# Projections ya and sb of a mixer formed with channels on partitions, with no transposition behind them

## The chip, the cores and the metric

The kernel runs on one core of a Trainium2 chip. The metric is the device time of one execution in microseconds, as the median of several runs. A core has TensorE for matrix products (PE in the profile, its weight loads PEld), VectorE (DVE), ScalarE (ACT), GpSimd (POOL) and SyncE (SP, which here only issues DMAs). Each takes its own instructions in order, and they wait for one another through semaphores.

## What is computed

Two blocks run one after the other on 256 tokens of width 1024, all in float32. The first is two layers of feed-forward, hybrid mixer, feed-forward; the second is one layer of attention and feed-forward. The change touches the mixer alone, which runs twice. Cut to what matters:

```python
def hybrid_mixer(u, ...):                      # u: 256 x 1024, normalised
    proj = u @ w_in                            # 1024 x 14336
    xa, ya, q, k, v, g, sb, sc, sh, gates = jnp.split(proj, cuts, axis=-1)
    xa = causal_depthwise_conv(xa, lru_conv_w) + lru_conv_b
    ha = rg_lru(xa, ...)                       # a linear recurrence along the tokens
    oa = (ha * jax.nn.gelu(ya)) @ w_lru_out
    ret = retention(q, k, v, positions)
    ob = (jax.nn.silu(g) * ret) @ w_ret_out
    oc = (sb * causal_depthwise_conv(sc * sh, sc_conv_w)) @ w_sc_out
    ga, gb, gc = jnp.split(jax.nn.sigmoid(gates), 3, axis=-1)
    return (ga * oa + gb * ob + gc * oc) @ w_out
```

The recurrence and the convolutions run along the tokens, channel by channel, and the results `ha * gelu(ya)` and `sb * conv(...)` are contracted over channels by the next weights. Both want the channels on the partitions and the tokens along the free axis.

## The kernel before

**Products in three parts.** Every float32 operand is held as a high part and a low part (`split`, L201 and L202, and for weights `convert`, L133 on ACT and L134 on DVE), and a product is three matmuls, high by high, high by low and low by high (`mm3`, L165 to L167). The weights come in 334 groups of 128 x 2048 by DMA into `raw` (three buffers), and are turned into `wh` and `wl` (five buffers each) in halves of 1024 columns.

**Projections with tokens on partitions.** `proj` takes one tile t of 128 tokens: the normalised activations `uh[t]`, `ul[t]`, which lie with the model width on partitions, are the stationary operand (128 x 128), and 512 columns of weights stream past them. Eight steps k over the width, three matmuls each, fill one PSUM bank `c` (two banks) of 128 tokens x 512 channels. The factor 1/rms of each token, `r2[t]`, is one number for each partition there, and is applied as the bank is read out.

**Turning to channels.** What is wanted with channels on partitions is turned. xa, sc and sh go through PE transposes (`transp`, L209). ya and sb go through `flip`: after the read-out into `yat` or `sbt`, DVE transposes 16 blocks for each 128 x 512, each of 32 rows by 4 x 32 columns (L224).

**Order.** The mixer goes: xa (four groups of weights), ya (four), sc and sh in two halves (eight), sb (four), the product with `w_lru_out` (four), the first gates, the product with `w_sc_out`, the second gates, then q, k, v and the retention. `later(n, fn)` holds work back until n steps of `mm3` more have been written; so `lru_half(0)` comes 8 steps and `lru_half(1)` 32 steps after ya, and the four strips of a `flip` come 5 (ya) or 28 (sb) steps after the read-out, two steps apart. `lru_half` makes a short convolution on ACT and DVE (`xc`, L446 and L448), then small float32 matmuls on it (L456), sigmoids (L459), the recurrence (L471), the product with ya (L473) and the split. From what is written a framework makes the final order of each engine's queue: it estimates when each instruction can start, and lets one that was written later go ahead of one that it takes to be still waiting. In the trace the conversions of weights run ahead of their use in this way.

Of the kernel before, what the change touches and what calls it, by code (L numbers as in the profile page):

```python
# [11 lines left out]
F32 = mybir.dt.float32  # L12
F32R = mybir.dt.float32r
I32 = mybir.dt.int32
AF = mybir.ActivationFunctionType
ALU = mybir.AluOpType
AX = mybir.AxisListType

P = 128
# [6 lines left out]
NEG = -1e30  # L26
CONV = 2
WSTEP = 2
WY = 5
WR = 6  # L30
WG = 8
WL0 = 8
WL1 = 32
WS0 = 5
WS1 = 12
WSB = 28
WMA = 14
WMB = 28
WMC = 18
# [6 lines left out]
S5 = 12  # L46
S6 = 32
WARM = 12
NRAW = 3
NW = 5  # L50
NGN = 3
# [21 lines left out]
def build(ctx: ExitStack, tc: tile.TileContext, a: dict, plan: list):  # L73
    nc = tc.nc
    V, A, G, T = nc.vector, nc.scalar, nc.gpsimd, nc.tensor

    def pool(name, bufs, **kw):
        return ctx.enter_context(tc.tile_pool(name=name, bufs=bufs, **kw))

    const = pool("const", 1)  # L80
    rawp = pool("raw", NRAW)
    wp = pool("w", NW)
# [5 lines left out]
    psC = pool("psc", 2, space=bass.MemoryType.PSUM)  # L88
# [12 lines left out]
    ident = const.tile([P, P], F32, name="ident")  # L101
# [1 line left out]
    G.memset(mhalf, -0.5)  # L103
    junk = const.tile([P, D], mybir.dt.bfloat16, name="junk")
    x = [const.tile([P, D], F32, name=f"x{t}") for t in range(2)]
    uh = [const.tile([P, 8, P], F32R, name=f"uh{t}") for t in range(2)]
    ul = [const.tile([P, 8, P], F32R, name=f"ul{t}") for t in range(2)]
    cst = const.tile([P, L, 12, 8], F32, name="cst")
    cos = const.tile([P, 2, P], F32, name="cos")
    sin = const.tile([P, 2, P], F32, name="sin")  # L110
# [1 line left out]
    lsz2 = const.tile([P, L, 8], F32, name="lsz2")  # L112
    tab = const.tile([33, 16], F32, name="tab")
    const.tile([P, 16], F32, name="even")
    r2 = [None, None]
    count = [0]
    pend = []
# [2 lines left out]
    def b4(name, dt=F32):  # L120
        return b4p.tile([P, D], dt, tag="b4", name=name)

    def b2(name, dt=F32):
        return b2p.tile([P, 512], dt, tag="b2", name=name)
# [4 lines left out]
    def tpbank(name="tp"):  # L129
        return psT.tile([P, 512], F32, tag="tp", name=name)  # L130
# [16 lines left out]
    def fetch(dst, src):  # L147
        with tc.issue_after(tail[0].ins if hasattr(tail[0], "ins") else tail[0]):
            nc.sync.dma_start(dst, src)
# [14 lines left out]
    def mm3(ps, xh, xl, wh, wl, first, last):  # L164
        T.matmul(ps, xh, wh, start=first, stop=False)  # L165
        T.matmul(ps, xh, wl, start=False, stop=False)  # L166
        T.matmul(ps, xl, wh, start=False, stop=last)  # L167
        count[0] += 1
        while pend and pend[0][0] <= count[0]:
            pend.pop(0)[1]()  # L170

    def later(n, fn):
        due = count[0] + n
        i = len(pend)
        while i and pend[i - 1][0] > due:
            i -= 1
        pend.insert(i, (due, fn))
# [22 lines left out]
    def split(hi, lo, src):  # L200
        A.copy(hi, src)  # L201
        V.tensor_tensor(lo, src, hi.bitcast(F32), ALU.subtract)  # L202
# [15 lines left out]
    def flip(dst, src, n, wait, done=None):  # L218

        sv = src[:, :n * P].rearrange("p (k n) -> p k n", n=P)  # L220

        def strip(q):
            for j in range(4):
                V.transpose(dst[32 * j:32 * j + 32, :, 32 * q:32 * q + 32], sv[32 * q:32 * q + 32, :, 32 * j:32 * j + 32])  # L224
            if q == 3 and done:
                done()

        for q in range(4):
            later(wait + q * WSTEP, lambda q=q: strip(q))
# [33 lines left out]
    def win(name, l, c0, n=512):  # L263
        kn = 2048 // n
        return [grp(name, l, k, kn, c0, n) for k in range(0, 8, kn)]

    def wout(name, l, k0, nk):
        return [grp(name, l, k, 2, 0, D) for k in range(k0, k0 + nk, 2)]

    def proj(gs, t, n=512, n0=0, nn=None):  # L270
        nn = n if nn is None else nn
        ps = psC.tile([P, 512], F32, tag="c", name="c")[:, :nn]
        kn = 2048 // n
        for k in range(8):
            wh, wl = gs[k // kn]
            sl = slice(n0, n0 + nn)
            mm3(ps, uh[t][:, k, :], ul[t][:, k, :], wh[:, k % kn, sl], wl[:, k % kn, sl], k == 0, k == 7)
        return ps

    def new_o():  # L280
# [2 lines left out]
    def acc_out(o, gs, xh, xl, first, last):  # L283
        for gi, (wh, wl) in enumerate(gs):
            for j in range(2):
                k = 2 * gi + j
                for n in range(2):
                    sl = slice(n * 512, n * 512 + 512)
                    mm3(o[:, sl], xh[:, k, :], xl[:, k, :], wh[:, j, sl], wl[:, j, sl],
                        first and k == 0, last and k == 2 * len(gs) - 1)  # L290
# [108 lines left out]
    def mixer(l, gpost, gpre):  # L399
        W = "w_mix_in"  # L400

        def chunk_tok(c0, n, cb):
            gs = [win(W, l, c0 + 512 * c) for c in range(n)]
            for t in range(2):
                for c in range(n):
                    cb(c, t, proj(gs[c], t))

        def chunks(c0, n, cb):
            for c in range(n):
                gs = win(W, l, c0 + 512 * c)  # L410
                for t in range(2):
                    cb(c, t, proj(gs, t))

        def ch(tile_):
            return tile_.rearrange("p (k s) -> p k s", s=S)
# [14 lines left out]

        wab = gp.tile([P, 2, 8, 64], F32, tag="gain", name="wab")
        fetch(wab, a["wab"][l])
        chunk_tok(0, 2, xa_cb)

        def col(row, k):
            return cst[:, l, row, k:k + 1]

        lru = []
        ya = [None, None]
# [35 lines left out]
            split(h, lo, rr)  # L475
            lru.append((h, lo))

        def ya_cb(c, t, ps):
            if ya[c] is None:
                ya[c] = ch(b4(f"ya{c}"))  # L480
            tmp = b2("yat")
            A.activation(tmp, ps, AF.Gelu_apprx_tanh, scale=r2[t])  # L482
            flip(ya[c][:, :, t * P:(t + 1) * P], tmp, 4, WY)

        chunks(1024, 2, ya_cb)
        later(WL0, lambda: lru_half(0))
        later(WL1, lambda: lru_half(1))

        pt = [None, None]
        for c in range(2):  # L490
            scs = [None, None]
            gs = win(W, l, 9216 + 512 * c)
# [4 lines left out]
            gs = win(W, l, 10240 + 512 * c)  # L497
# [4 lines left out]
        for c in range(2):  # L502
            z = ch(b4(f"z{c}"))
            for j in range(4):
                k = 4 * c + j
                A.activation(z[:, j, :], pt[c][:, j, :], AF.Copy, scale=col(SW + 2, k))
                for s in range(1, 3):
                    V.scalar_tensor_tensor(z[:, j, s:], pt[c][:, j, :S - s], col(SW + 2 - s, k), z[:, j, s:],
                                           ALU.mult, ALU.add)
            gs = win(W, l, 8192 + 512 * c)  # L510
            h, lo = ch(b4(f"sh{c}", F32R)), ch(b4(f"sl{c}", F32R))
            for t in range(2):
                tmp = b2("sbt")
                A.activation(tmp, proj(gs, t), AF.Copy, scale=r2[t])

                def cb(tp, z=z, h=h, lo=lo, sl=slice(t * P, (t + 1) * P)):
                    V.tensor_tensor(z[:, :, sl], tp, z[:, :, sl], ALU.mult)
                    split(h[:, :, sl], lo[:, :, sl], z[:, :, sl])
                sbT = b2("sbT").rearrange("p (k n) -> p k n", n=P)
                flip(sbT, tmp, 4, WSB, lambda cb=cb, sbT=sbT: cb(sbT))  # L520
            sco.append((h, lo))

        acc = [None, None]
# [137 lines left out]
        gs = wout("w_mix_out", l, 0, 8)  # L661
# [266 lines left out]
    warm = tpbank("warm")  # L928
    for i in range(WARM):
        T.transpose(warm[:, :P], ident, ident)  # L930
# [110 lines left out]
def _weights(inputs, plan):  # L1041
    w2 = inputs["w_in_2"]
    perm = np.arange(w2.shape[2])
    halves = np.arange(512).reshape(2, 4, 64).transpose(1, 0, 2).reshape(-1)
    for c in (0, 768, 1280):
        perm[c:c + 512] = c + halves
    src = dict(inputs)
    src["w_in_2"] = w2[:, :, perm]
    w = np.empty((NG, P, 2048), np.float32)
    for i, (name, l, k0, kn, c0, n) in enumerate(plan):  # L1050
        blk = src[name][l][k0 * P:(k0 + kn) * P, c0:c0 + n]
        w[i] = blk.reshape(kn, P, n).transpose(1, 0, 2).reshape(P, 2048)
    return w


def _program(inputs):
    import concourse.bacc as _bacc

    nc = _bacc.Bacc("TRN2", target_bir_lowering=False, num_devices=1)
    arrays = _layout(inputs)  # L1060
    args = {n: nc.dram_tensor(n, v.shape, mybir.dt.from_np(v.dtype), kind="ExternalInput").ap()
            for n, v in arrays.items()}
    args["wts"] = nc.dram_tensor("wts", (NG, P, 2048), F32, kind="ExternalInput").ap()
    args["out"] = nc.dram_tensor("out", (S, D), F32, kind="ExternalOutput").ap()
    plan = []
    with tile.TileContext(nc) as tc:
        build(tc, args, plan)
    arrays["wts"] = _weights(inputs, plan)
    return nc, arrays, plan
# [9 lines left out]
```

## Time and profile before

| what | value |
|---|---|
| median of 3 runs | 2027.7 us (2027.6 to 2027.93) |
| profiled execution: its time, its span | 2028.99 us, 2027.2 us |
| PE busy | 1972.9 us (97%), 9170 matmuls |
| DVE busy | 1668.2 us (82%) |
| ACT busy | 1037.3 us (51%) |
| weights read from HBM | 367.05 MB, mean 182 GB/s |

The span is the time from the first to the last instruction in the profile. A matmul's busy time overlaps that of the next, so how fast PE works is read from the distance between the starts of two matmuls rather than from their durations. PEclk is the share of full speed at which TensorE's clock was granted.

### The profile page before, as it was taken

How to read it: one execution, taken by the hardware profiler on the slowest of the kernel's cores; microseconds unless marked ns; L12 is line 12 of the kernel's file. 1: busy time of each engine (PE TensorE's matmuls, PEld its weight loads, DVE VectorE, ACT ScalarE, POOL GpSimd, SP SyncE). 2: the span in 40 equal slices, each digit the busy share in tenths (PEclk: the TensorE clock that was granted, in tenths of full speed). 3: DMA queues.
4: the chain of work that ended last, by engine and by line, in shares of the span. 5: the costliest groups of instructions: out<-in, count | busy, mean ns of one | idle time of the engine just before them, and what ended most of it. 6: DMA issues, size and time to landing. Idle time of an engine off the chain costs nothing.

```text
span 2027.2 us, 24429 instructions
## 1 busy us (share of the span) xinstructions
PE 1972.9 (97%) x9170; PEld 1623.8 (80%) x9170; DVE 1668.2 (82%) x2893; ACT 1037.3 (51%) x1384; POOL 58.5 (3%) x116
## 2 busy tenths in 40 slices
PE   9999999999999999999999999999999999999997
PEld 7778868788788888888887778887888888787886
DVE  7989789776877998988878995777789897679997
ACT  6444676444444543544466843454454445654553
POOL 0000000000010000000000000000010000010000
PEclk9999999999999999999999999999999999999999
DMA  6555533654445454555653546435545556424542
GB/s 250 192 208 198 187 134 137 244 189 166 166 160 212 173 207 181 198 197 187 239 190 107 183 184 220 169 115 199 205 166 208 198 207 207 161 94 149 220 183 102
DMA packets 56319, 369.72 MB, mean 182 GB/s; under 512 B 6582, under 2 KB 8886, under 8 KB 13704
## 3 DMA queue, kind: packets, MB, share of 16 engines
q1 hardware_dynamic: 56200, 368.16, 49.9%
q8 instruction: 72, 1.18, 0.2%
q14 instruction: 47, 0.39, 0.1%
HBM read 367.05 MB, written 1.08 MB: 182 GB/s over the span
## 4 chain that ended last, share of the span: by engine, by line
PE 65%; DVE 24%; ACT 4%; issue 3%; DMA 2%; POOL 0%; SPq 0%; DVEq 0%; POOLq 0%; ACTq 0%
PE c L165 13%; PE c L166 13%; PE c L167 13%; DVE ht L224 9%; DVE wl L134 8%; PE o L166 7%; PE o L167 7%; PE o L165 7%; DMA raw<-wts 2%; ACT wh L133 2%; DVE sbT L224 2%; DVE ya L224 2%; PE tp L209 2%; PE tp L456 1%; PE pv L762 1%
## 5 line engine op out<-in xcount | busy, mean ns | idle before, releaser
L134 DVE TENSOR_TENSOR wl<-raw,wh 128x1024 fp32r<-128x1024 f32 (+1 forms) x670 | 787.7, 1216 | 171.9 <-ACT wh L133 168.7
L133 ACT CAST wh<-raw 128x1024 fp32r<-128x1024 f32 (+1 forms) x670 | 670.0, 1046 | 336.4 <-PE c L167 163.6
L165 PE MATMUL c<-wh,uh 128*128 128x512 f32 (+1 forms) x1912 | 740.4, 387 | 14.4 <-DVE v L608 5.6
L166 PE MATMUL c<-wl,uh 128*128 128x512 f32 (+1 forms) x1912 | 734.9, 384 | 11.1 <-DVE wl L134 11.1
L167 PE MATMUL c<-wh,ul 128*128 128x512 f32 (+1 forms) x1912 | 734.3, 384 | 0.0
L165 PEld LDWEIGHTS c<-wh,uh 128*128 128x128 f32 x1912 | 363.2, 190 | 89.5 <-DVE v L608 6.5
L166 PEld LDWEIGHTS c<-wl,uh 128*128 128x128 f32 x1912 | 363.4, 190 | 82.5 <-DVE wl L134 12.6
L167 PEld LDWEIGHTS c<-wh,ul 128*128 128x128 f32 x1912 | 362.9, 190 | 71.1 <-issue 1.2
L224 DVE STREAM_TRANSPOSE ht<-sil 32x128 f32<-32x128 f32 (+1 forms) x768 | 223.9, 292 | 10.7
L224 DVE STREAM_TRANSPOSE ht<-sg 32x128 f32<-32x128 f32 x256 | 77.5, 303 | 3.5
L224 DVE STREAM_TRANSPOSE ht<-mh 32x128 f32<-32x128 f32 x256 | 77.5, 303 | 3.4
L195 POOL TENSOR_SCALAR ms<-ss 128x1 f32<-128x1 f32 x52 | 21.9, 421 | 1936.8 <-ACT junk L190 1915.6
L306 ACT ACTIVATE sil<-c,r 128x512 f32<-128x512 f32 (+1 forms) x48 | 31.3, 651 | 41.0 <-PE c L167 40.9
L311 DVE SCALAR_TENSOR_TENSOR sil<-c,r,sil 128x512 f32<-128x512 f32 (+1 forms) x48 | 33.7, 702 | 13.3 <-PE c L167 13.1
L224 DVE STREAM_TRANSPOSE ya<-yat 32x128 f32<-32x128 f32 x128 | 38.7, 302 | 6.0 <-ACT yat L482 4.3
L224 DVE STREAM_TRANSPOSE sbT<-sbt 32x128 f32<-32x128 f32 x128 | 38.8, 303 | 2.0
L197 POOL TENSOR_TENSOR r<-ms,mhalf 128x1 f32<-128x1 f32 x54 | 35.4, 656 | 4.5
L201 ACT CAST h2h<-ht 128x512 fp32r<-128x512 f32 x10 | 6.2, 623 | 52.2 <-DVE ht L224 52.2
L166 PE MATMUL o<-wl,h1h 128*128 128x512 f32 x80 | 31.4, 392 | 0.2 <-DVE wl L134 0.2
L166 PE MATMUL o<-wl,h4h 128*128 128x512 f32 x80 | 31.2, 390 | 0.0
L165 PE MATMUL o<-wh,h3h 128*128 128x512 f32 x80 | 31.2, 390 | 0.0
L166 PE MATMUL o<-wl,h3h 128*128 128x512 f32 x80 | 31.2, 390 | 0.0
(334 smaller groups left out, 2434.1 us busy)
## 6 DMA issues: line engine op xcount, KB each, us to landing
raw<-wts SPq DMA_DIRECT2D x332, 1024.0 KB, 4.8
tb<-row SPq DMA_DIRECT2D x8, 384.0 KB, 5.4
gain_ffn_post_g<-gains SPq DMA_DIRECT2D x4, 512.0 KB, 7.6
dec<-dec SPq DMA_DIRECT2D x4, 384.0 KB, 5.6
gain_ffn_pre_g<-gains SPq DMA_DIRECT2D x3, 512.0 KB, 8.5
x<-x SPq DMA_DIRECT2D x2, 512.0 KB, 5.7
raw<-wts SPq DMA_DIRECT2D x4, 256.0 KB, 5.5
raw<-wts SPq DMA_DIRECT2D x2, 512.0 KB, 6.4
```

The costliest lines, as they stand in the source:

```text
L133: A.copy(wh[:, sl], raw[:, sl])
L134: V.tensor_tensor(wl[:, sl], raw[:, sl], wh[:, sl].bitcast(F32), ALU.subtract)
L165: T.matmul(ps, xh, wh, start=first, stop=False)
L166: T.matmul(ps, xh, wl, start=False, stop=False)
L167: T.matmul(ps, xl, wh, start=False, stop=last)
L195: G.tensor_scalar(ms, ss, mul / n, mul * EPS, ALU.mult, ALU.add)
L197: G.tensor_tensor(r, ms, mhalf, ALU.pow)
L209: T.transpose(tp[:, j, :], src[:, (b + j) * P:(b + j + 1) * P], ident)
L224: V.transpose(dst[32 * j:32 * j + 32, :, 32 * q:32 * q + 32], sv[32 * q:32 * q + 32, :, 32 * j:32 * j + 32])
L306: A.activation(sil[t], ps, AF.Silu, scale=r2[t])
L311: V.scalar_tensor_tensor(sil[t], ps, r2[t], sil[t], ALU.mult, ALU.mult)
L456: T.matmul(ps[b:b + 64, j, :], wab[b:b + 64, g, 4 * c + j0 + j, :], xc[b:b + 64, j0 + j, :], start=True, stop=True)
```

## The change

For ya and sb the operands trade places: 128 columns of weights become the stationary operand, and 256 tokens (both tiles, from one buffer that now holds both) stream past. The result has channels on partitions. Each bank `c` then holds two blocks of 128 channels by 256 tokens. The factor 1/rms now varies along the free axis, so it is laid out once in each mixer as a row that is the same on all partitions (`rrow`), by a product of a matrix of ones with a diagonal. DVE applies it as it reads the bank out. `mm3c` counts as half a step, so the numbers given to `later` keep their sense.

```diff
-    uh = [const.tile([P, 8, P], F32R, name=f"uh{t}") for t in range(2)]
-    ul = [const.tile([P, 8, P], F32R, name=f"ul{t}") for t in range(2)]
+    uhb = const.tile([P, 2, 8, P], F32R, name="uh")
+    ulb = const.tile([P, 2, 8, P], F32R, name="ul")
+    uh, ul = [uhb[:, t] for t in range(2)], [ulb[:, t] for t in range(2)]
...
+    ones = const.tile([P, P], F32, name="ones")
+    G.memset(ones, 1.0)
+    rrow = const.tile([P, 2, P], F32, name="rrow")
...
+    def mm3c(ps, xh, xl, wh, wl, first, last):
+        T.matmul(ps, wh, xh, start=first, stop=False)
+        T.matmul(ps, wl, xh, start=False, stop=False)
+        T.matmul(ps, wh, xl, start=False, stop=last)
+        tick(0.5)
...
+    def scale_rows():
+        tp = tpbank("rb")
+        for t in range(2):
+            dg = b2("dg")[:, :P]
+            A.activation(dg, ident, AF.Copy, scale=r2[t])
+            T.matmul(tp[:, t * P:(t + 1) * P], ones, dg, start=True, stop=True)
+        A.copy(rrow.rearrange("p t n -> p (t n)"), tp[:, :2 * P])
+
+    def per_token(ps):
+        return rrow.unsqueeze(1).to_broadcast([P, 2, 2, P])
+
+    def proj_ch(gs, j0):
+        ps = psC.tile([P, 512], F32, tag="c", name="c").rearrange("p (j t n) -> p j t n", j=2, t=2)
+        for j in range(2):
+            sl = slice((j0 + j) * P, (j0 + j + 1) * P)
+            for k in range(8):
+                wh, wl = gs[k // 4]
+                mm3c(ps[:, j], uhb[:, :, k, :], ulb[:, :, k, :], wh[:, k % 4, sl], wl[:, k % 4, sl], k == 0, k == 7)
+        return ps
...
+        later(ROWS, scale_rows)
         chunk_tok(0, 2, xa_cb)
...
-        def ya_cb(c, t, ps):
-            if ya[c] is None:
-                ya[c] = ch(b4(f"ya{c}"))
-            tmp = b2("yat")
-            A.activation(tmp, ps, AF.Gelu_apprx_tanh, scale=r2[t])
-            flip(ya[c][:, :, t * P:(t + 1) * P], tmp, 4, WY)
-
-        chunks(1024, 2, ya_cb)
+        for c in range(2):
+            gs = win(W, l, 1024 + 512 * c)
+            ya[c] = ch(b4(f"ya{c}"))
+            for j in range(0, 4, 2):
+                y = ya[c][:, j:j + 2, :].rearrange("p j (t n) -> p j t n", n=P)
+                ps = proj_ch(gs, j)
+                V.tensor_tensor(y, ps, per_token(ps), ALU.mult)
+                A.activation(y, y, AF.Gelu_apprx_tanh)
...
-            for t in range(2):
-                tmp = b2("sbt")
-                A.activation(tmp, proj(gs, t), AF.Copy, scale=r2[t])
-
-                def cb(tp, z=z, h=h, lo=lo, sl=slice(t * P, (t + 1) * P)):
-                    V.tensor_tensor(z[:, :, sl], tp, z[:, :, sl], ALU.mult)
-                    split(h[:, :, sl], lo[:, :, sl], z[:, :, sl])
-                sbT = b2("sbT").rearrange("p (k n) -> p k n", n=P)
-                flip(sbT, tmp, 4, WSB, lambda cb=cb, sbT=sbT: cb(sbT))
+            for j in range(0, 4, 2):
+                ps = proj_ch(gs, j)
+                sbt = b2("sbt").rearrange("p (j t n) -> p j t n", j=2, t=2)
+                V.tensor_tensor(sbt, ps, per_token(ps), ALU.mult)
+                zj = z[:, j:j + 2, :].rearrange("p j (t n) -> p j t n", n=P)
+                V.tensor_tensor(zj, sbt, zj, ALU.mult)
+                split(h[:, j:j + 2, :], lo[:, j:j + 2, :], z[:, j:j + 2, :])
```

`scale_rows` is held back 28 steps (`ROWS = 28`), which falls into the last of the four xa projections. The rest of the diff makes room in memory (a smaller scratch area for DMAs that no transfer of this kernel uses, and one filler tile).

## Rows read from the trace of the kernel before

**Rows 1.** The page, busy time, share of the span and instructions of each engine.
```profile
PE 1972.9 (97%) x9170; PEld 1623.8 (80%) x9170; DVE 1668.2 (82%) x2893; ACT 1037.3 (51%) x1384; POOL 58.5 (3%) x116
```

**Rows 2.** Timeline of PE, feed-forward: start us, us, instruction; 512 columns, then 256.
```profile
30.08 0.39 PE L165 MATMUL c<-wh,uh 128*128 128x512 f32 x1
...
53.88 0.39 PE L165 MATMUL c<-wh,uh 128*128 128x512 f32 x1
...
163.18 0.28 PE L165 MATMUL c<-wh,uh 128*128 128x256 f32 x1
...
174.58 0.28 PE L167 MATMUL c<-wh,ul 128*128 128x256 f32 x1
```

**Rows 3.** Timeline of PE, first layer, after ya: around the small products of `lru_half`.
```profile
254.44 0.39 PE L167 MATMUL c<-wh,ul 128*128 128x512 f32 x1
258.01 1.97 PE L456 MATMUL tp<-xc,wab 64*64 64x256 f32 x8 [3.18 <-DVE xc L448]
...
264.73 0.39 PE L165 MATMUL c<-wh,uh 128*128 128x512 f32 x1
...
293.98 1.08 PE L456 MATMUL tp<-xc,wab 64*64 64x256 f32 x8 [0.93 <-DVE xc L448]
...
298.95 1.94 PE L456 MATMUL tp<-xc,wab 64*64 64x256 f32 x16
300.82 0.50 PE L165 MATMUL c<-wh,uh 128*128 128x512 f32 x1
```

**Rows 4.** Timeline of PE, both layers: the stop behind the product with `w_lru_out`.
```profile
354.72 0.39 PE L165 MATMUL c<-wh,uh 128*128 128x512 f32 x1
...
363.57 0.39 PE L166 MATMUL c<-wl,uh 128*128 128x512 f32 x1
...
1186.52 0.39 PE L165 MATMUL c<-wh,uh 128*128 128x512 f32 x1
1190.91 0.80 PE L166 MATMUL c<-wl,uh 128*128 128x512 f32 x1 [4.01 <-DVE wl L134]
...
1196.51 0.40 PE L167 MATMUL c<-wh,ul 128*128 128x512 f32 x1
```

**Rows 5.** Timeline of DVE, first layer, from ya to the first stop.
```profile
248.07 5.04 DVE L224 STREAM_TRANSPOSE ya<-yat 32x128 f32<-32x128 f32 x16
...
257.27 3.24 DVE L448 SCALAR_TENSOR_TENSOR xc<-xa,cst,xc 128x253 f32<-128x253 f32 x8
```

**Rows 6.** Windows: us, busy PE, PEld, DVE, ACT, POOL (x), PEclk, DMA share, GB/s.
```profile
311.00:333.00 22.00, 21.98 (x102) 17.97 (x101) 20.99 (x29) 17.37 (x26) 0.00 (x0) 1.00 0.47 177
333.00:355.00 22.00, 22.00 (x98) 17.98 (x96) 21.11 (x61) 8.44 (x10) 0.00 (x0) 1.00 0.28 96
...
1191.00:1196.00 5.00, 5.00 (x12) 3.94 (x13) 4.90 (x8) 0.00 (x0) 0.00 (x0) 0.50 0.61 193
```

**Rows 7.** Groups by line and shape: count, busy us, mean ns, idle before.
```profile
L224 DVE STREAM_TRANSPOSE sbT<-sbt 32x128 f32<-32x128 f32 x128 | 38.8, 303 | 2.0
...
L549 DVE TENSOR_TENSOR sg<-o,sg 128x512 f32<-128x512 f32 x16 | 11.0, 689 | 22.3 <-ACT sg L547 22.3
...
L514 ACT ACTIVATE sbt<-c,r 128x512 f32<-128x512 f32 x8 | 5.5, 693 | 3.8 <-PE c L167 3.8
...
L166 PEld LDWEIGHTS c<-wl,uh 128*128 128x128 f32 x1912 | 363.4, 190 | 82.5 <-DVE wl L134 12.6 <-issue 2.6
```

**Rows 8.** Timeline of PE: the small products whose kind stands nearest to the ones.
```profile
141.86 1.02 PE L677 MATMUL bps<-oh,tab 33*8 33x512 f32 x2
...
301.39 0.60 PE L209 MATMUL tp<-ident,scs 128*128 128x128 f32 x4
301.75 0.48 PE L167 MATMUL c<-wh,ul 128*128 128x512 f32 x1
```

**Rows 9.** Timeline of DVE, first layer, where sb is formed.
```profile
323.93 6.40 DVE L508 SCALAR_TENSOR_TENSOR z<-pt,cst,z 128x255 f32<-128x255 f32 x16 [0.96 <-ACT z L506]
330.24 3.49 DVE L134 TENSOR_TENSOR wl<-raw,wh 128x1024 fp32r<-128x1024 f32 x3
```

## Prediction on record

> **What bounds the kernel now.** I read the page's busy times first, then PE's timeline, then DVE's timeline in the places where PE stopped. PE is busy for 97% of the span and DVE for 82% [rows 1]. The question is where PE stands still, and for whom.
>
> The full pace of PE comes from the starts. From 30.08 to 53.88 us there are 105 matmuls of 512 columns, so one takes 23.80 / 105 = 0.2267 us. From 163.18 to 174.58 there are 96 of 256 columns, 95 steps, so 0.1200 us each [rows 2]. A mixer is a long run at this pace with two large stops, the same two in each layer.
>
> *Stop one, after ya.* PE's last matmul before it starts at 254.44, the small products of `lru_half(0)` wait 3.18 us for the convolution `xc` on DVE, and the stream is back at full pace at 264.73 [rows 3]. In these 10.29 us lie 7 matmuls of 512 columns (1.59 us) and 16 small products, which take 1.87 us when nothing is in their way (298.95 to 300.82 [rows 3]). The stop costs 10.29 - 1.59 - 1.87 = 6.8 us. DVE is late because it turns ya: a block of 16 transpositions takes 5.04 us, and the second part of `xc` starts only at 257.27 [rows 5]. Layer two has the like stop.
>
> *Stop two, behind `w_lru_out`.* The first matmul of the gates starts at 354.72, the second waits for `wl`, and the pace is back at 363.57: 8.85 us with 13 matmuls, so 8.85 - 2.95 = 5.9 us lost. In layer two it is 9.99 us with 14 matmuls, 6.8 us lost [rows 4]. Here DVE is busy 21.11 of 22 us from 333 to 355 [rows 6], most of it with turning sb.
>
> Part of each price is the clock. After the wait in layer two the granted clock is 0.50 for the next 5 us [rows 6], the lower of TensorE's two levels (1.2 GHz of 2.4); PE had been idle for 4.01 us [rows 4]. The end of the chain of work runs along PE, so what PE gets back here, the kernel gets back.
>
> The two stops come to 2 x 6.8 + 5.9 + 6.8 = 26.3 us. `lru_half(1)` waits another 0.93 us for DVE [rows 3], in each layer.
>
> **The change part by part.**
>
> *Transpositions removed.* 128 for ya and 128 for sb, 303 ns each [rows 7]: 77.6 us of DVE in all. 16 in a row take 5.04 us [rows 5], so a mixer has 8 such blocks, 40 us of DVE, in exactly the two stretches where PE then waits for DVE.
>
> *Matmuls.* A chunk of 512 channels took 48 matmuls of 512 columns, 48 x 0.2267 = 10.88 us. It now takes 96 of 256 columns, 96 x 0.1200 = 11.52 us. There are four chunks in each mixer, eight in all: 8 x 0.64 = +5.1 us, all on the path. The 0.1200 us were measured on operands of the same type, each with a weight load of its own. What the row lacks is that the streamed side now lies in two pieces of 128. From below that costs nothing; from above, each piece would go like a transposition of 128 columns, (301.75 - 301.39) / 4 = 0.09 us [rows 8], 0.18 for two, and 46 us more in all. I take nothing, since type, width and loads are those of the 256-column row; the upper end goes with rival D.
>
> A weight load shows 190 ns [rows 7], more than the 120 ns between two matmuls, so loads run beside other work of PE. This is where the Trainium skill speaks against the change. Its page "TensorE: Matmul & The Clock Gate" (section "Measured speedup vs the span model") says that a weight load overlaps matmuls in flight only where it uses other rows of the array, and all rows are used here. In its section "LDWEIGHTS" the load of 128 columns takes 128 / 1.2 = 107 ns. With 384 more loads that is an estimate of 41 us more by the page against my 5.1. The trace does not bear it out, since 107 ns of streaming and 107 ns of load would not fit into 120.
>
> *Read-out.* Each of 16 banks is read by a DVE multiplication with the row `rrow`; the nearest row is 689 ns for 128 x 512 out of PSUM [rows 7], so 11.0 us of DVE. This replaces the read by ACT, 693 ns [rows 7]. For sb that frees ACT; for ya, ACT still has the Gelu, now out of SBUF. Multiplying into z and splitting keep number and size. DVE's balance is -77.6 + 11.0 = -66.6 us. ACT is busy 51% [rows 1] and sets nothing here.
>
> *Where the read-out queues.* It stands in DVE's order among the conversions of weights. Two banks `c` exist, so a read-out may start up to 8 x 2 x 3 x 0.1200 = 5.76 us late before PE waits. Around ya, four blocks of transpositions (20.2 us) leave DVE and four read-outs (2.8 us) come, so it should be on time. Around sb it is tighter: from 311 to 333 us DVE is busy 20.99 of 22 [rows 6], and four read-outs (2.8 us) come into this stretch, with z's products and splits moving up from behind. I take no wait here, and price one below.
>
> *The rows of 1/rms.* Two products with ones in each mixer, four in all, on PE. The nearest rows are float32 products of 33 rows x 512 columns, 1.02 / 2 = 0.51 us, and the transpositions of 128 columns at 0.09 us [rows 8]. I take 0.25 us each, since it has float32 operands but a quarter of the columns: 1.0 us, with ends 0.4 and 2.0. They come in the last quarter of xa, one ACT pass after a factor that xa's own read-out needs anyway. If ACT were late with the diagonal, PE would lose about 1 us at each.
>
> *Conversions of weights.* `proj_ch` goes through all eight k in 2.88 us instead of 5.44, so the second group of a window is wanted earlier and both are given back later. Five buffers stand against two in use, and no group of weights or DMA is added or moved. I take nothing. This cover would go if DVE fell a whole window behind.
>
> *Sum.* -26.3 (both stops gone, their low clock with them) + 5.1 + 1.0 = -20.2 us. The 0.93 us in front of `lru_half(1)` I leave standing. On the profiled span that is 2027.2 - 20.2 = 2007.0 us. The execution with the profile took 2028.99, 1.8 more than its span, and the median of the runs without it is 2027.7, 0.5 more than that span. So I take 2027.7 - 20.2 = 2007.5 us.
>
> **The rivals.**
>
> *A. As summed: both stops go.* 2007.5 us, its own range 2001 to 2014: below if the 0.93 us go too and the products with ones are at their lower end, above if a wait of some 3 us appears in each layer. Chance 0.60.
>
> *B. One of the stops stays.* DVE may remain the last to arrive behind `w_lru_out`, because at sb it was full already and some 8.3 us of read-outs, products and splits (12, at the 689 ns of [rows 7]) move up into it; or the framework puts the conversions that DVE now reaches early ahead of `xc`, and stop one stays. For it: 20.99 of 22 us busy. Against it: behind sb PE works 21.8 us on four groups, for which DVE owes 8 conversions of 3.49 / 3 us [rows 9], 9.3 us. Then 12.7 or 13.7 us are not won: about 2021 us, and 2014 to 2024 with half a stop. Chance 0.20.
>
> *C. PE waits for read-outs, and the kernel is slower.* At sb the 16 steps of z occupy DVE for 6.40 us in one piece, followed by 3.49 us of conversions [rows 9]. A read-out that falls in behind both is 9.9 us late, 4.1 us beyond its cover of 5.76. With the low clock behind it this is a stop of the size of stop two, 6.3 us. Two such in each layer cost 25 us and turn the sum: 2007.5 + 25.2 = 2033 us. From four stops in all it is slower than before; three leave it about equal. For it: the order of DVE's queue is an estimate, and stop two shows that it can be wrong by 4 us. Against: z's steps could then start earlier, since DVE is freed before. Chance 0.11.
>
> *D. Weight loads do not hide.* If each of 384 more loads cost its 190 ns [rows 7], PE would need 73 us more in place of the 5.1: 2007.5 + 68 = 2075 us. The 0.1200 us of the 256-column rows speak against it. The two-piece price above, 46 us, would end near 2048 in the same way. This is the rule of the skill cited above. Chance 0.03 for both.
>
> *E. Nothing moves.* The stops shrink by what the matmuls cost, because the next wait in each place, ACT's sigmoids behind `xc` or the DMA of weights, ends only shortly before DVE's did: 2025 to 2030 us. Chance 0.06.
>
> **How the numbers follow.** A difference under 0.2%, 4 us, is about what a measurement of this kernel cannot tell from no change. Faster: A and B, and 0.01 of E, 0.81. Same: the rest of E (0.05) and the part of C with three stops (0.02), 0.07. Slower: C with four or more (0.09) and D (0.03), 0.12. The range for 8 in 10 takes A and B whole, 2001 to 2024; C, D and E, 0.20, lie above it but for E's edge.
>
> **What the profile after would show.** Rows of L224 for ya and sb are gone, and 768 matmuls of 256 columns are new with starts 0.120 us apart (A) or 0.3 (D). PE's wait for L448 after ya and for `wl` at the gates behind `w_lru_out` is gone and the granted clock there is 1.00; if one stands, B. Waits of PE in front of a projection's first matmul, ended by the new multiplication on DVE, show C. DVE's busy time falls to about 1602 us. The prediction is wrong if PE gets idle in new places for 12 us or more, or if the 256-column pace with two pieces is above 0.146 us, at which 768 of them eat the whole gain.

## The result, and the profile after

| | before | after |
|---|---|---|
| median, us | 2027.82 (2027.6 to 2028.3, 4 runs) | 2005.64 (2004.06 to 2007.12, 4 runs) |
| profiled execution: its time, its span | 2028.99, 2027.2 | 2004.06, 2002.3 |

The ratio of the runs is 0.9893, with a 95% interval of 0.9881 to 0.9905. That is 22.2 us less, where the forecast was 20.2 less (2007.5 us).

The page's busy times of the changed kernel come first, in the columns of [rows 1].

```profile
PE 1964.2 (98%) x9562; PEld 1638.3 (82%) x9562; DVE 1601.3 (80%) x2653; ACT 1033.9 (52%) x1382; POOL 59.0 (3%) x117
```

DVE lost 66.9 us of work. PE's share rose to 98%, though it has 392 matmuls more in a shorter span.

Next is PE's timeline of the changed kernel at seven places in order of time: the products with ones, the new 256-column matmuls, the first products of `lru_half(0)`, those of `lru_half(1)`, a transposition of sc and sh, the first gates, and the values of the second pair of heads.

```profile
224.98 0.61 PE L299 MATMUL rb<-dg,ones 128*128 128x128 f32 x4
225.34 0.48 PE L169 MATMUL c<-wh,uh 128*128 128x512 f32 x1
...
236.09 0.28 PE L182 MATMUL c<-ul,wh 128*128 128x256 f32 x1
...
237.89 0.28 PE L182 MATMUL c<-ul,wh 128*128 128x256 f32 x1
...
257.61 1.95 PE L492 MATMUL tp<-xc,wab 64*64 64x256 f32 x16
259.49 0.51 PE L169 MATMUL c<-wh,uh 128*128 128x512 f32 x1
...
290.27 1.08 PE L492 MATMUL tp<-xc,wab 64*64 64x256 f32 x8 [0.94 <-DVE xc L484]
...
316.77 1.14 PE L222 MATMUL tp<-ident,scs 128*128 128x128 f32 x8 [0.48 <-ACT pt L454]
...
352.74 0.39 PE L169 MATMUL c<-wh,uh 128*128 128x512 f32 x1
352.96 0.39 PE L170 MATMUL c<-wl,uh 128*128 128x512 f32 x1
...
542.89 0.50 PE L169 MATMUL c<-wh,uh 128*128 128x512 f32 x1 [2.40 <-DVE v L642]
```

Both large stops are gone. Where [rows 3] has a wait of 3.18 us in front of `lru_half(0)`, 16 small products now go through in 1.88 us without one. Where [rows 4] has 4.4 us between the first two matmuls of the gates in layer two, there are 0.22 in the rows above, and no wait in layer two either. The smaller waits stay: 0.94 us for `xc` and the one for the values. One of 0.48 us for a copy by ACT is new; it comes with sb, since `e2_sb_alone` below has it and `e1_ya_alone` does not. The 256-column matmuls start (237.89 - 236.09) / 15 = 0.120 us apart.

DVE's timeline of the changed kernel shows why. Its lines answer to [rows 5] and [rows 9].

```profile
246.50 0.69 DVE L520 TENSOR_TENSOR ya<-c,rrow 128x512 f32<-128x512 f32 x1 [0.85 <-PE c L182]
247.10 4.81 DVE L484 SCALAR_TENSOR_TENSOR xc<-xa,cst,xc 128x255 f32<-128x255 f32 x12
...
321.65 0.69 DVE L553 TENSOR_TENSOR z<-sbt,z 128x512 f32<-128x512 f32 x1
322.26 0.69 DVE L551 TENSOR_TENSOR sbt<-c,rrow 128x512 f32<-128x512 f32 x1
...
335.96 4.63 DVE L138 TENSOR_TENSOR wl<-raw,wh 128x1024 fp32r<-128x1024 f32 x4
```

The convolution `xc` is done in one piece and finished at 251.9, 5.7 us before PE wants it. Before, its second part started only at 257.27 [rows 5]. Behind sb, DVE turns to the conversions at once. The windows of the changed kernel, in the columns of [rows 6], hold the stretch around stop one, the formation of sb, the product behind it and the first gates.

```profile
249.00:265.00 16.00, 16.00 (x98) 12.18 (x98) 8.13 (x13) 10.49 (x15) 0.00 (x0) 1.00 0.42 160
311.00:331.00 20.00, 19.52 (x164) 19.25 (x163) 19.01 (x31) 12.42 (x21) 0.00 (x0) 1.00 0.26 98
331.00:354.00 23.00, 23.00 (x103) 19.05 (x103) 16.68 (x17) 10.89 (x13) 0.00 (x0) 1.00 0.74 274
354.00:364.00 10.00, 10.00 (x46) 8.29 (x45) 4.87 (x5) 5.15 (x7) 0.00 (x0) 1.00 0.53 210
```

While sb is formed DVE is still full (19.01 of 20 us), as it was (20.99 of 22). Behind it, it has 16.68 of 23 to do where it had 21.11 of 22 [rows 6], and at the gates the clock is 1.00.

**PE's account.** I went through all starts of PE's timeline and added what the distances exceed full pace (0.2267 us for 512 columns, 0.120 for 256, 0.117 for a small product of `lru_half`, 0.09 for a transposition, 0.12 for the rest). I call this the loss. Each mixer is taken from the same matmul to the same matmul in every kernel; in the kernel before these are 197 to 640 us and 1030 to 1500. In the two mixers the loss was 21.6 + 24.5 = 46.1 us before and is 7.9 + 10.8 = 18.7 us after: 27.4 us won. The two stops make up 26.4 of them: above what the same stretch loses in the changed kernel, the one after ya had cost 6.4 and 7.3 us in the two layers and the one behind `w_lru_out` 5.9 and 6.8. The 256-column matmuls cost 5.1 and the products with ones 2 x 0.36 = 0.7, so the mixers give 27.4 - 5.1 - 0.7 = 21.6 us.

Behind the second mixer, where the code did not change, the loss went from 27.3 to 22.6. In the profiles of the experiments below it lies between 22.7 and 27.0 there, without a relation to the edits. I count that as variation between executions; 2.9 of the 4.7 us lie at a single wait for `wl` near the end, of 3.92 us with the low clock behind it before and of 2.72 us at the full clock after. In front of the first mixer 1.1 us were added. These three sum to 25.2 us, and the two profiled spans differ by 24.9.

Two smaller things in the mixers nearly cancel. The new wait for ACT costs 0.9 us in all. The stops at the values cost 1.6 us less, all of it in the first layer, and not because the wait there shrank: it is 2.40 us where the kernel before has 2.41.

```profile
550.79 0.50 PE L165 MATMUL c<-wh,uh 128*128 128x512 f32 x1 [2.41 <-DVE v L608]
```

In the kernel before the granted clock fell to 0.50 behind this wait (0.56 on average from 551 to 553 us); in the changed kernel it stayed at 1.00.

### The profile page after: what moved, and what is told of

Same layout as the page of the kernel before. It is cut to its first block, busy times and chain, and to the rows that moved or that the text cites. A ratio compares the mean times of both kernels' runs of the same rounds, so it can differ in the third digit from the quotient of the medians.

```text
span 2002.3 us, 24972 instructions
## 1 busy us (share of the span) xinstructions
PE 1964.2 (98%) x9562; PEld 1638.3 (82%) x9562; DVE 1601.3 (80%) x2653; ACT 1033.9 (52%) x1382; POOL 59.0 (3%) x117
## 4 chain that ended last, share of the span: by engine, by line
PE 75%; DVE 16%; ACT 4%; issue 2%; DMA 2%; POOL 0%; SPq 0%; DVEq 0%; POOLq 0%; ACTq 0%
PE c L169 14%; PE c L170 14%; PE c L171 14%; PE o L170 8%; PE o L171 8%; PE o L169 8%; DVE ht L237 7%; DVE wl L138 6%; PE tp L222 2%; ACT wh L137 1%; DMA raw<-wts 1%; PE c L182 1%; PE c L181 1%; PE c L180 1%; PE pv L796 1%
## 5 line engine op out<-in xcount | busy, mean ns | idle before, releaser
L169 PE MATMUL c<-wh,uh 128*128 128x512 f32 (+1 forms) x1784 | 687.9, 386 | 12.3 <-DVE v L642 5.6
L170 PE MATMUL c<-wl,uh 128*128 128x512 f32 (+1 forms) x1784 | 683.0, 383 | 3.5 <-DVE wl L138 3.5
L171 PE MATMUL c<-wh,ul 128*128 128x512 f32 (+1 forms) x1784 | 682.3, 382 | 0.1
L170 PEld LDWEIGHTS c<-wl,uh 128*128 128x128 f32 x1784 | 337.5, 189 | 69.2 <-DVE wl L138 5.0
L208 POOL TENSOR_SCALAR ms<-ss 128x1 f32<-128x1 f32 x52 | 22.3, 428 | 1911.4 <-ACT junk L203 1890.2
L180 PE MATMUL c<-uh,wh 128*128 128x256 f32 x256 | 72.8, 284 | 0.0
L181 PE MATMUL c<-uh,wl 128*128 128x256 f32 x256 | 72.7, 284 | 0.0
L182 PE MATMUL c<-ul,wh 128*128 128x256 f32 x256 | 72.5, 283 | 0.0
L180 PEld LDWEIGHTS c<-uh,wh 128*128 128x128 f32 x256 | 49.2, 192 | 0.1
L181 PEld LDWEIGHTS c<-uh,wl 128*128 128x128 f32 x256 | 49.2, 192 | 0.1
L182 PEld LDWEIGHTS c<-ul,wh 128*128 128x128 f32 x256 | 49.1, 192 | 0.0
```

Of the source, the lines that this page charges most:

```text
L180: T.matmul(ps, wh, xh, start=first, stop=False)
L181: T.matmul(ps, wl, xh, start=False, stop=False)
L182: T.matmul(ps, wh, xl, start=False, stop=last)
```

## The experiments

Each was timed in five rounds beside the kernel before on the same chip (median of before 2027.63 us for the first four, 2028.91 for the second four, 2029.67 for the last two).

**One part alone.** In `e1_ya_alone` ya has the new form and sb the old, in `e2_sb_alone` the other way round:

```diff
 # e1_ya_alone, against the changed kernel
-            for j in range(0, 4, 2):
-                ps = proj_ch(gs, j)
...
+            for t in range(2):
+                tmp = b2("sbt")
+                A.activation(tmp, proj(gs, t), AF.Copy, scale=r2[t])
...
+                flip(sbT, tmp, 4, WSB, lambda cb=cb, sbT=sbT: cb(sbT))
```

> Only ya is formed with channels on partitions; sb is formed and turned as before. If each stop goes because DVE has less to do in the stretch in front of it, the stop after ya is gone (13.7 us less in two layers), the stop behind w_lru_out stays at 6 to 7 us a layer, and PE pays 4 x 0.64 = 2.6 us for ya's matmuls and under 1 us for the rows of 1/rms: about 2017.5 us. If it is the total load of DVE that counts, wherever it is taken off, both stops shrink by half. If the gain comes from sb alone, through the read-out that ACT no longer does, the time is about 2031 us.

> Only sb is formed with channels on partitions; ya is turned as before. By the load in front of each stop, the stop after ya stays at 6.8 us a layer and the one behind w_lru_out is gone (12.7 us less), against 2.6 us for sb's matmuls and under 1 us for the rows: about 2018.5 us. The two parts together should give what the whole change gave, 22 us. If the gain comes from ya alone, about 2031 us.

ya alone: 2014.56 us, ratio 0.9929 (0.9916 to 0.9941). sb alone: 2018.4 us, 0.9949 (0.9937 to 0.9962). The gains of 13.1 and 9.2 us add up to 22.3, against 22.2 for the whole. PE's timeline of `e1_ya_alone` has the second stop still, and the first one gone:

```profile
259.66 1.94 PE L494 MATMUL tp<-xc,wab 64*64 64x256 f32 x16
...
353.08 0.39 PE L171 MATMUL c<-wh,uh 128*128 128x512 f32 x1
357.45 0.79 PE L172 MATMUL c<-wl,uh 128*128 128x512 f32 x1 [3.98 <-DVE wl L140]
```

In `e2_sb_alone` PE waits 4.50 us in front of `lru_half(0)`, and no wait stands at the gates:

```profile
261.77 1.97 PE L494 MATMUL tp<-xc,wab 64*64 64x256 f32 x8 [4.50 <-DVE xc L486]
```

So each stop belongs to the turning in front of it; neither total load nor one of the parts carries the whole. ya alone won 3 us more than expected. Its loss in the mixers is 13.8 + 15.1 = 28.9 us, 17.2 less than before, where 13.7 were expected. The stop after ya gives the 13.7; the rest is 2.2 us at the two stops in front of `v` and 1.1 us of a shorter second stop in layer two, neither of which the sum has.

**The transposition left out, the old form kept.** In `e3_no_turning` a copy stands in place of 16 transpositions, so the blocks of ya and sb are not turned.

```diff
 # against the kernel before, for ya and sb
-                flip(sbT, tmp, 4, WSB, lambda cb=cb, sbT=sbT: cb(sbT))
+                unturned(sbT, tmp, 4, WSB, lambda cb=cb, sbT=sbT: cb(sbT))
...
+        def one():
+            V.tensor_copy(dst, sv)
+            if done:
+                done()
+        later(wait + 3 * WSTEP, one)
```

> The kernel before, with ya and sb still formed with tokens on partitions and read out by ACT, but each turning of 128 x 512 (16 transpositions, 5.04 us) replaced by one copy of about 0.6 us on DVE, so that the transposition is left out of the computation. If DVE's transpositions cause both stops, they go without any change of the matmuls: 2027.8 - 26.3 = 2001.5 us, some 5 us below the changed kernel. If it was the other form of the projection or the read-out by DVE that reordered the queues in a lucky way, the stops stay and the time is near 2027 us.

2000.52 us (1997.33 to 2001.18), ratio 0.9856 (0.9843 to 0.987). The matmuls, ACT's read-out and the products all have their old form, and both stops are gone. PE's timeline of this kernel has the first small products without a wait, at their full pace, and the first two matmuls of the gates 0.23 us apart:

```profile
255.75 1.94 PE L466 MATMUL tp<-xc,wab 64*64 64x256 f32 x16
...
349.16 0.39 PE L165 MATMUL c<-wh,uh 128*128 128x512 f32 x1
349.39 0.39 PE L166 MATMUL c<-wl,uh 128*128 128x512 f32 x1
```

The 5.1 us between it and the changed kernel are about what the new form costs PE (5.1 + 0.7 by the account). The other form of the projection brings no gain of its own.

**The transpositions put back.** `e4_turn_idle` is the changed kernel with as many transpositions, into a tile that nobody reads.

```diff
                 A.activation(y, y, AF.Gelu_apprx_tanh)
+                flip(b2("idle").rearrange("p (k n) -> p k n", n=P), ya[c][:, j:j + 2, :].rearrange("p j s -> p (j s)"), 4, WY)
...
                 V.tensor_tensor(zj, sbt, zj, ALU.mult)
+                flip(b2("idle").rearrange("p (k n) -> p k n", n=P), sbt.rearrange("p j t n -> p (j t n)"), 4, WSB)
```

> The changed kernel, with the same number of transpositions on DVE put back at the same delays, into a tile that nobody reads. If DVE's time in these stretches is the cause, the stops come back and the cost of the matmuls stays: 2005.6 + 26 = about 2032 us, above the kernel before, and more if DVE's new read-outs are held up behind them. If the order or the other form is the cause, the time stays near 2006 us.

2043.89 us, ratio 1.0072 (1.0059 to 1.0086): slower than before, and 38 us above the changed kernel where 26 were expected. PE's timeline has both stops again, larger, and with further waits beside them:

```profile
260.69 1.09 PE L494 MATMUL tp<-xc,wab 64*64 64x256 f32 x8 [2.58 <-ACT ya L523]
...
265.62 1.97 PE L494 MATMUL tp<-xc,wab 64*64 64x256 f32 x8 [3.84 <-DVE xc L486]
...
353.16 0.50 PE L172 MATMUL o<-wl,lh 128*128 128x512 f32 x1 [1.68 <-DVE wl L140]
...
367.98 0.50 PE L172 MATMUL c<-wl,uh 128*128 128x512 f32 x1 [3.65 <-DVE wl L140]
```

The loss in the mixers is 25.7 + 28.7 = 54.4 us, 36 above the changed kernel. Here DVE has the transpositions and the read-outs on top, and PE has waits that the kernel before does not have: a second one in front of `lru_half(0)`, which the profile puts down to the Gelu of ya, and one inside the product with `w_lru_out`. The direction was as expected; that the price would grow was not in my sum. Whether the 11 us of read-outs on top or the order of DVE's queue made it grow was not separated.

**DVE relieved by other means.** `e9_turn_on_pe` is the kernel before with ya and sb turned by PE.

```diff
-            flip(ya[c][:, :, t * P:(t + 1) * P], tmp, 4, WY)
+            to_ch(ya[c], tmp, t)
...
-                flip(sbT, tmp, 4, WSB, lambda cb=cb, sbT=sbT: cb(sbT))
+                transp(tmp, 4, lambda b, m, tp, cb=cb: cb(tp), WT)
```

> The kernel before, with ya and sb turned by PE transposes (as xa is) in place of DVE. This takes the same load off DVE as the change does, by another means: both stops should go (26.3 us). The price on PE is 64 transpositions at 0.09 us, 5.8 us, and some 0.15 us for each of 16 interruptions, 2.4 us: 2027.8 - 18 = about 2010 us. If what counts is the form with channels on partitions and not DVE's relief, or if the two PSUM banks for transposes hold PE up, the time stays at 2020 us or above.

2007.7 us, ratio 0.9893 (0.9876 to 0.9909), the same ratio as the change. The window of the product with `w_lru_out`, in the columns of [rows 6], has 13.14 of 22 us of work for DVE, and PE has no wait there or at the gates:

```profile
333.00:355.00 22.00, 22.00 (x100) 18.20 (x100) 13.14 (x13) 8.94 (x11) 0.00 (x0) 1.00 0.54 198
```

Channels on partitions are one way among others to take the turning off DVE. On this kernel it costs PE about as much as turning on PE does.

**The read-outs doubled.** `e8_read_twice` reads each bank of ya and sb a second time.

```diff
+                V.tensor_tensor(b2("idle").rearrange("p (j t n) -> p j t n", j=2, t=2), ps, per_token(ps), ALU.mult)
                 V.tensor_tensor(sbt, ps, per_token(ps), ALU.mult)
```

> The changed kernel with every bank read out by DVE twice, the first time into a tile that nobody reads: 16 x 0.69 = 11 us more of DVE, in exactly the place of the new read-outs. If these stand under cover, as the prediction took it, nothing moves by more than 3 us. If PE's next banks hang on them, each of the 16 makes PE wait 0.69 us and more, and the time is 2017 us or above.

2006.05 us, ratio 0.989 (0.9876 to 0.9903): nothing moves. The cover of a read-out, one other bank of 5.76 us, is wide enough for twice its length, but at sb only just. The second bank of sb is the tightest. In the changed kernel these are its read-out on DVE and PE's first matmul that needs the bank again:

```profile
322.26 0.69 DVE L551 TENSOR_TENSOR sbt<-c,rrow 128x512 f32<-128x512 f32 x1
325.19 0.28 PE L180 MATMUL c<-uh,wh 128*128 128x256 f32 x1
```

In `e8_read_twice` they are its second reading and the like matmul:

```profile
323.70 0.68 DVE L553 TENSOR_TENSOR sbt<-c,rrow 128x512 f32<-128x512 f32 x1
324.52 0.36 PE L180 MATMUL c<-uh,wh 128*128 128x256 f32 x1
```

The first has 2.2 us to spare (325.19 - 322.95), the second 0.14 (324.52 - 324.38); layer two is the same.

**The streamed side in one piece.** `e5_side_by_side` lays the tokens of both tiles next to each other.

```diff
-    uhb = const.tile([P, 2, 8, P], F32R, name="uh")
+    uhb = const.tile([P, 8, 2, P], F32R, name="uh")
...
-                mm3c(ps[:, j], uhb[:, :, k, :], ulb[:, :, k, :], wh[:, k % 4, sl], wl[:, k % 4, sl], k == 0, k == 7)
+                mm3c(ps[:, j], uhb[:, k], ulb[:, k], wh[:, k % 4, sl], wl[:, k % 4, sl], k == 0, k == 7)
```

> The changed kernel with the tokens of both tiles side by side, so that the 256 columns that stream past lie in one piece. If two pieces of 128 cost TensorE nothing, as the prediction took it, the matmuls still start 0.120 us apart and the time stays at 2005.6 us within 2 us. If each piece costs a start of its own, PE gets faster here, by up to 46 us if it were the whole of the upper bound.

2004.58 us, ratio 0.9887 (0.9873 to 0.99), and the median distance of starts is 0.120 us in both kernels. Two pieces cost nothing that can be seen.

**Halves.** `e6_halves` cuts each matmul into two of 128 columns.

```diff
-            for k in range(8):
-                wh, wl = gs[k // 4]
-                mm3c(ps[:, j], uhb[:, :, k, :], ulb[:, :, k, :], wh[:, k % 4, sl], wl[:, k % 4, sl], k == 0, k == 7)
+            for t in range(2):
+                for k in range(8):
+                    wh, wl = gs[k // 4]
+                    mm3c(ps[:, j, t], uhb[:, t, k, :], ulb[:, t, k, :], wh[:, k % 4, sl], wl[:, k % 4, sl], k == 0, k == 7)
```

> The changed kernel with each matmul of 256 columns cut into two of 128, each with a weight load of its own: 1536 matmuls and loads in place of 768. If loads hide completely, whatever the length of the stream, two halves take as long as the whole and the time stays near 2006 us. If a load sets a floor, it is seen in the distance of the starts: at the 0.09 us of the transpositions of 128 columns, 1536 x 0.09 - 768 x 0.12 = +46 us, about 2052 us; at the 0.107 us that the Trainium skill gives for a load of 128 columns, +72 us, about 2078 us; at the 0.190 us that the profile shows for one load, +200 us.

2169.57 us, ratio 1.0698 (1.0684 to 1.0713), so 164 us above the changed kernel. Two things come together, and PE's timeline of this kernel shows both:

```profile
234.43 0.28 PE L182 MATMUL c<-ul,wh 128*128 128x128 f32 x1
...
237.78 0.28 PE L182 MATMUL c<-ul,wh 128*128 128x128 f32 x1
...
337.20 0.46 PE L181 MATMUL c<-uh,wl 128*128 128x128 f32 x1
...
409.90 0.41 PE L182 MATMUL c<-ul,wh 128*128 128x128 f32 x1
```

From 234.43 to 237.78 there are 30 steps of 0.112 us, nearly the 0.120 of twice the columns. So these matmuls have a floor, and it is set by something that does not get shorter with the stream. At 0.112, 1536 matmuls take 172 us, 80 more than the 92 us of 768 at 0.120. From 337.20 to 409.90, 337 steps of 0.2157 us on average follow: the lower clock, in both layers, which is 2 x 337 x 0.104 = 70 us more. It starts with a stop of 5.8 us for a copy by ACT, which accounts for another 12 in two layers. Together that is 162 of the 164 us.

**Carried further.** `e7_ret_pe` applies the same reasoning to the wait for `v`, which stands behind DVE's turning of the first two retention heads: PE turns their results in place of DVE. `e10_ret_pe_late` is also meant to hold back `lru_half(1)`.

```diff
 # e7_ret_pe, against the changed kernel
-                dve_split(rh[:, t], rl[:, t], sg, 4, WR)
+                if h < 2:
+                    tr_split(rh[:, t], rl[:, t], sg, 4, WR)
+                else:
+                    dve_split(rh[:, t], rl[:, t], sg, 4, WR)
...
 # e10_ret_pe_late, in addition
-WL1 = 32
+WL1 = 38
```

> The changed kernel, with the results of the first two retention heads turned by PE in place of DVE: 64 transpositions of DVE fewer in each mixer, 16 of PE more. If the rule holds that PE stops where DVE is loaded in front of it, the stop of 4 to 5 us a layer at the values of the second pair of heads goes, against 16 x 0.09 = 1.4 us and some 0.5 us for the interruptions: 5 to 6 us less, about 2000 us. If the DMA of weights ends that wait anyway, the time is the same or 3 us more.

> The kernel with the first two retention heads turned by PE, and with the second half of the recurrence held back by 38 steps in place of 32, so that its convolution on DVE has 4 us more until PE wants it. If the 0.93 us in front of it are the lateness of DVE alone, they go, about 2 us in two layers: 1998 us. If the wait moves along with the work, the time stays at 1999.8 us.

`e7_ret_pe`: 1999.83 us, ratio 0.9862 (0.9849 to 0.9876), the fastest kernel that computes everything, 5.8 us below the changed one. From 495 to 550 us PE has no wait left; its loss in the mixers is 5.6 + 6.1 = 11.7 us, 7.0 below the changed kernel. `e10_ret_pe_late`: 2002.58 us, ratio 0.987 (0.9855 to 0.9885), no gain. The wait for `xc` is 0.96 us in place of 0.93, but the products were not held back. The first of them in `e7_ret_pe`:

```profile
289.85 1.08 PE L492 MATMUL tp<-xc,wab 64*64 64x256 f32 x8 [0.93 <-DVE xc L484]
```

And in `e10_ret_pe_late`:

```profile
288.69 0.65 PE L492 MATMUL tp<-xc,wab 64*64 64x256 f32 x4 [0.96 <-DVE xc L484]
```

The mixers begin at 198.0 and 197.2 us, so that is 91.9 and 91.5 us into the mixer: the products start no later, and only stand in smaller groups. The framework's order undid the delay, and whether 4 us more for DVE would remove the wait stays open.

## Why the prediction was right

**The gain.** The step was 26.3 us for two stops in each layer, with their low clock. The stops gave 26.4 us, of 27.4 by which the loss of PE in the mixers fell, and the two parts show them going one by one. For the stop after ya the prediction took the 6.8 us of layer one for both layers; it was 6.4 and 7.3, and that the sum fits so closely is partly luck. That DVE's turning was the cause is shown from three sides: without it the stops go in the old form (`e3_no_turning`), with it they are back in the new form (`e4_turn_idle`), and turning on PE gives the same ratio (`e9_turn_on_pe`).

**The cost on PE.** 5.1 us was worked out from 0.120 us for a matmul of 256 columns; the changed kernel has 0.120, with two pieces or one (`e5_side_by_side`). The products with ones took 0.36 us in each mixer, 0.7 us in place of 1.0.

**DVE's balance.** 66.6 us less were expected and 66.9 measured, with 681 and 688 ns for a read-out where 689 were taken.

**The cover.** The read-outs were costed at nothing, and no wait of PE for one stands in the changed kernel. Rival C did not come true, but it was no empty fear: at the second bank of sb 2.2 us were left, and `e8_read_twice` uses up all but 0.14. C took the 16 steps of z as one piece in front of a read-out; in the changed kernel DVE has them in pieces of 8, 3 and 5, with read-outs and products between them, which the prediction did not foresee. It was right that DVE is full while sb is formed; the load that moved up was paid behind it, where 21.11 us of work in 22 [rows 6] became 16.68 in 23.

**Rivals B and E** fell too: neither stop stayed, and in neither place did another wait follow. **Rival D** was refuted at 256 columns: the starts are 0.120 us apart. `e6_halves`, with half the columns, has a floor of 112 ns. By the section "LDWEIGHTS (loading the stationary operand)" of the Trainium skill's page "TensorE: Matmul & The Clock Gate", a load takes its columns divided by 1.2, in ns, which is an estimate of 107 ns for 128 columns. The 112 ns agree with that within 5. The rule that a load overlaps a matmul in flight only where it uses other rows of the array, which the prediction cites, stands in the section "The mechanism" of the same page of the Trainium skill. It doesn't hold in this trace: loads on all 128 rows and streams of 256 columns together take 120 ns, and 256 further columns alone take 107 (0.2267 - 0.1200 us [rows 2]). That the 112 ns are the load is only argued from the agreement; no run here changed the load alone. The transpositions of [rows 8] speak against it as a general price, for each has a load of 128 columns too and they start 0.09 us apart, though they are another kind of matmul. These are their loads, on PEld in the kernel before:

```profile
301.17 0.59 PEld L209 LDWEIGHTS tp<-ident,scs 128*128 128x128 f32 x4
```

**What was off.** The forecast of 2007.5 us was 1.9 above the median. The account of the mixers, -27.4 + 5.1 + 0.7 = -21.6 us, explains all but 0.6 of the 22.2, less than the runs of one kernel differ (2004.06 to 2007.12). The prediction had neither the 0.9 us of the new wait for ACT nor the 1.6 us at the values; that they nearly cancel is luck. What would have been wrong is the reverse sum: the same load put back cost 38 us, not 26.

## What to carry to other kernels

Read the distance between the starts of the busiest engine's instructions, find the few places where it is exceeded, and ask what the engine waited for did in the 20 us before; here 77.6 us of transpositions taken off DVE were worth 26, and each half was worth the stop behind it. To change the form of a product is not a gain by itself: price it by rows of the very shape it will have, and compare it with other means of taking off the same load. A stop is worth looking for again after each change, since the next one (the wait for `v`) gave way to the same reasoning for another 6 us.

## What the runs showed of the hardware

The low clock can last without any stop. In `e6_halves` PE is busy for the whole of the following windows, and yet the granted clock stays at 0.50 (1.2 of 2.4 GHz) in the first, 24 us after the stop; it is at 1.00 in the second, when matmuls of 512 columns have come back. Layer two shows the same behind the like stop.

```profile
360.00:366.00 6.00, 6.00 (x30) 6.00 (x29) 0.00 (x0) 0.00 (x0) 0.00 (x0) 0.50 0.00 0
...
417.00:423.00 6.00, 6.00 (x28) 4.98 (x27) 0.94 (x1) 2.01 (x2) 0.00 (x0) 1.00 0.31 130
```

Before that stop, the same matmuls of 128 columns ran for 43 us at the full clock (from 227.81 to 271.03 us). So an order of short matmuls that keeps its clock may not get it back after a stop.

Nor does the length of a wait alone tell whether the clock falls behind it. In `e1_ya_alone` the longer of the two waits for `v` leaves the granted clock at 1.00, and the shorter one does not (0.62 on average over the 4 us behind it). These are the two waits on PE's timeline, and then the windows behind them:

```profile
549.56 0.50 PE L171 MATMUL c<-wh,uh 128*128 128x512 f32 x1 [2.92 <-DVE v L646]
...
1373.52 0.50 PE L171 MATMUL c<-wh,uh 128*128 128x512 f32 x1 [2.08 <-DVE v L646]
```

```profile
549.50:553.50 4.00, 3.94 (x17) 3.29 (x18) 4.00 (x6) 2.95 (x4) 0.00 (x0) 1.00 0.95 313
1373.50:1377.50 4.00, 3.98 (x11) 3.15 (x12) 3.55 (x4) 3.10 (x4) 0.00 (x0) 0.62 1.02 354
```

The same holds between kernels: 2.41 us before with the fall, 2.40 us after without it. The stretch at the low clock cost 1.7 us there, so two executions can differ by that much through this alone.

A matmul of 256 columns takes 0.120 us and two of 128 take 0.223, each with a load of its own.
